# Sums of a layer norm on another engine, centring from PSUM, and a new order of weights and products around it

## The chip, the cores and the metric

One NeuronCore of a Trainium2 chip runs the whole program. The metric is device time in microseconds (us) of one execution. The engines are TensorE (PE, matrix products, its weight loads are PEld), VectorE (DVE), ScalarE (ACT), GpSimd (POOL) and the DMA queues; SP and POOL issue the DMAs here. Each engine runs its own instruction stream in order, and semaphores hold an instruction until what it needs is there.

## The reference

The program is a two-layer decoder trunk on 528 positions (16 learned tokens and 512 inputs) of width 1024. What matters for the change is the shape of a layer:

```python
for l in range(2):
    h = layer_norm(ALPHA * h + 0.5 * swiglu(h, ffn1_wg[l], ffn1_wu[l], ffn1_wd[l]), g[l,0], b[l,0])
    mix = short_conv(h, ...) if l == 0 else forgetting_attention(h, w_q, w_o, k, v, c)
    h = layer_norm(ALPHA * h + mix, g[l,1], b[l,1])
    h = layer_norm(ALPHA * h + 0.5 * swiglu(h, ffn2_wg[l], ffn2_wu[l], ffn2_wd[l]), g[l,2], b[l,2])
    if l == 0: k, v, c = shared_kv(h, kv_w, f_bias)
return h[:, 16:]

def layer_norm(x, g, b):
    mu = mean(x); var = mean((x - mu)**2)
    return (x - mu) * rsqrt(var + 1e-5) * g + b
```

All data are float32. There are six norms. The last one is written in another way and is not touched; the other five, in order of time, are called norm 1 to norm 5: after the first feed-forward block, after the convolution, after the second feed-forward block (its result feeds keys and values), after the third feed-forward block (its result feeds the queries), and after the attention.

## The kernel before, in words

**Layout.** Activations lie transposed: the 1024 features are 8 tiles of 128 partitions (`m` or `k` from 0 to 7), and the positions are the free axis, in two halves `h` of 264 columns in layer 0 and 256 in layer 1. The residual stream is the tile `y`. Every product is made of three float32r matmuls (L243 to L246): weights and activations are split into a high part, rounded on ScalarE (`wh` L132, `xh` L257), and a low part, the remainder, on VectorE (`wl` L134, `xl` L258). A contraction tile of one job is thus three matmuls, and after each the counter `tick` runs; `later(n, fn)` puts work of TensorE n such steps later.

**The order.** The instruction stream of TensorE is the order of the program text. The streams of the other engines are laid out ahead of time by a planner that goes by program order (an earlier line first), readiness in its own simulated time, and dependencies. `tc.high_priority(offset=600)` (L420) moves the end of a norm 600 instructions forward in that order; `tc.issue_after(ins)`, used by `behind` (L112), holds the instructions of the same engine behind `ins`.

**A norm.** `down` (L484) runs the products into `y`: `m` 0 to 2 of both halves, then `m` 3 to 7 of half 0, then `m` 3 to 7 of half 1; each product has 6 contraction tiles in norms 1, 3 and 4 and 8 in norms 2 and 5. Each is added to `y` on VectorE (L502). In `Norm.add` (L395) ScalarE squares the new row of `y`, and GpSimd adds the row to `s1` (L409) and its square to `s2` (L411); row 7 is not added there. `Norm.post` (L413) is placed `LAG[h]` steps behind the last product of its half: TensorE sums row 7 and `s1` into `pd`, and the square of row 7 and `s2` into `pv`, by matmuls with a constant matrix (L419). `finish` (L425) makes the variance `v` (L430), the inverse root `r` by eight VectorE instructions (`rsqrt`, L347), `b = -mean * r` (L434), and then for each pair of tiles `y * r` (L438) and `y + b` (L439), on ScalarE gain and bias (L442), and the split for what comes next (`made`: `xh`, `xl`).

**What comes next.** After norms 1 and 4 it is plain products (`Plain`): in norm 1's case the convolution's three projections `conv_u` (two jobs, `pcc` and `pcv`) and `conv_b` (`pcb`), in norm 4's the queries (`pq`). After norms 2, 3 and 5 it is a unit of gate and up weights, or of key and value weights, whose first 256 columns are computed directly (`Direct.half`, tiles `pc`) for one half after the other; the following units use a scheme with seven products in place of eight, for which sums of weights (L200 to L211) and of activations (`Mixed.sums`, L318) are made on VectorE. `xs.sums()` is held behind the first half's last split (L609). The first product that takes a weight sum of the second unit and `t2` writes `pb`.

**Early weights.** `ahead`, called when the first six products are out (L496), splits the first weights of the next stage; `to.early()`, at the end of `post(0)` (L423), splits more, with `wl` held behind the last split of half 0's activations (`newest`, L446). Buffers: 14 `xtile`s, 5 each of `wh` and `wl`, 3 raw weight buffers of 1 MB, 8 PSUM banks.

Of the kernel before, what the change touches and what calls it, by code (L numbers as in the profile page):

```python
# [34 lines left out]
LEAD = 3  # L35
LAG = (4, 5)
SOON = 600
# [9 lines left out]
def trunk_kernel(  # L47
# [63 lines left out]
    @contextmanager  # L111
    def behind(*after):  # L112


        with ExitStack() as stack:
            for ins in after or newest[-1:]:
                stack.enter_context(tc.issue_after(ins.ins))
            yield

    def split_w(src, shape, home=None):  # L120
# [11 lines left out]
        nc.scalar.copy(a, src)  # L132
        with behind():
            nc.vector.tensor_tensor(b, src, a.bitcast(F32), ALU.subtract)  # L134
# [34 lines left out]
    class Quads:  # L169
# [21 lines left out]
        def sums(self):  # L191
            if "s" in self.got:
                return
            self("a11")
            s = wp.tile([P, KD * P], F32, tag="ws", bufs=1, name="s")
            s = s.rearrange("p (j k n) -> p j k n", j=2, k=KH)
            self.got["s"] = s
            a11, a21, a22 = self.part(0, 0), self.part(1, 0), self.part(1, 1)
            with behind():
                nc.vector.tensor_tensor(s, a21, a22, ALU.add)  # L200
                nc.vector.tensor_tensor(a21, a11, a21, ALU.add)
                nc.vector.tensor_tensor(a11, a11, s, ALU.add)

        def __call__(self, name):
            if name not in self.got:
                if name[0] == "s":
                    self.sums()
                if name == "s4":
                    a12 = self.part(0, 1)
                    with behind():  # L210
                        nc.vector.tensor_tensor(a12, a12, self.part(0, 0), ALU.add)  # L211
# [135 lines left out]
    def rsqrt(v, r, a):  # L347
# [9 lines left out]
        nc.vector.scalar_tensor_tensor(a, v, -10.0 / 3, v, ALU.add, ALU.mult)  # L357
        nc.vector.scalar_tensor_tensor(r, a, 5.0, r, ALU.add, ALU.mult)


    class Norm:
        def __init__(self, layer, i, eps, to):
            self.layer, self.i, self.eps, self.to = layer, i, eps, to
            self.s1, self.s2, self.sq, self.early = {}, {}, {}, {}

# [29 lines left out]
        def add(self, h, m, gather):  # L395

            if h not in self.s2:
                self.early.setdefault(h, []).append((m, gather))
                return
            gather()  # L400
            yv = cols(y, h, self.layer)
# [4 lines left out]
            if m == KD - 1:  # L406
                self.sq[h] = sq
                return
            nc.gpsimd.tensor_tensor(  # L409
                self.s1[h], yv[:, 0, :] if m == 1 else self.s1[h], yv[:, m, :], ALU.add)  # L410
            nc.gpsimd.tensor_tensor(self.s2[h], self.s2[h], sq, ALU.add)  # L411

        def post(self, h):  # L413
# [6 lines left out]
            with tc.high_priority(offset=SOON):  # L420
                self.finish(h, pd, pv)
            if h == 0:
                self.to.early()  # L423

        def finish(self, h, pd, pv):  # L425
            yv = cols(y, h, self.layer)
            w = yv.shape[2]
            v = self.tmp(h, "v", 1)
            nc.scalar.activation(v, pd, AF.Square)
            nc.vector.scalar_tensor_tensor(v, pv, self.eps, v, ALU.add, ALU.subtract)  # L430
            r, a = self.tmp(h, "r", 1), self.tmp(h, "a", 1)
            rsqrt(v, r, a)
            b = self.tmp(h, "b", 1)
            nc.vector.scalar_tensor_tensor(b, pd, -1.0, r, ALU.mult, ALU.mult)  # L434
            rb, bb = (t.unsqueeze(1).broadcast_to([P, 2, w]) for t in (r, b))
            for m in range(0, KD, 2):
                ym = yv[:, m:m + 2, :]
                nc.vector.tensor_tensor(ym, ym, rb, ALU.mult)  # L438
                nc.vector.tensor_tensor(ym, ym, bb, ALU.add)  # L439
                for j in range(m, m + 2):  # L440
# [3 lines left out]
                        scale=vecs[:, c:c + 1], bias=vecs[:, 48 + c:49 + c])  # L444
                last = self.to.made(h, m)
            newest.append(last[1])  # L446

# [130 lines left out]
    class Direct:  # L578
# [6 lines left out]
        def half(self, h, finish):  # L585
            ps = {(j, m): psum(f"pc{j}{m}")[:, :self.w] for m in range(2) for j in range(2)}
            for n in range(2):
                for m in range(2):
                    wh, wl = self.quads(f"a{m + 1}{n + 1}")
                    for j in range(2):  # L590
                        gemms([(ps[j, m], (wh[:, j], wl[:, j]), self.xs[f"b{n + 1}{h + 1}"])],
                              range(KH), start=n == 0, stop=n == 1, chained=True)
            for m in range(2):
# [146 lines left out]
    w_in = [Weights(conv_w_in[0], 0, KD, j * D, KD) for j in range(3)]  # L740
    for j in (1, 2):
        w_in[j].home = {0: xtile}
    xc = Plain(0, lambda: (w_in[1](1), w_in[2](1), w_in[0](0)))
    ffn(0, ffn1_wg[0], ffn1_wu[0], ffn1_wd[0], 0, xs0, xc, ready=f1,
        ahead=lambda: (w_in[1](0), w_in[2](0)))

# [43 lines left out]

    for part, i, h in (
            (conv_u, 0, 0), (conv_u, 1, 0), (conv_b, 0, 0), (conv_u, 0, 1), (conv_b, 0, 1),
            (conv_u, 1, 1), (conv_b, 1, 0), (conv_b, 1, 1)):
        run([part(i, h)])
    for i in range(2, KD):
# [129 lines left out]
    q_w = Weights(attn_w_q[0], 0, KD, 0, H)  # L925
    q_w.home = {m: xtile for m in range(2)}
    xq = Plain(1, lambda: [q_w(m) for m in range(2, 5)])
    ffn(1, ffn1_wg[1], ffn1_wu[1], ffn1_wd[1], 3, xs2, xq, ahead=lambda: (q_w(0), q_w(1)))

# [126 lines left out]
    fetch(0)  # L1056
    project(range(2), [0])
    project(range(2, 5), [0])
    project(range(3), [1])
# [107 lines left out]
```

## Time and profile before

| | |
|---|---|
| median of 3 runs | 1938.0 us (1937.51 to 1941.57) |
| profiled execution, its own time | 1939.81 us |
| its span, first to last instruction | 1938.0 us |
| mean granted TensorE clock | 0.992 |
| TensorE busy | 1882.2 us (97%), 14467 matmuls |
| VectorE busy | 1399.1 us (72%) |
| ScalarE busy | 875.1 us (45%) |
| GpSimd busy | 136.6 us (7%) |

The profile is one execution. A line of the timeline gives start and duration in us, engine, line of the kernel, operation, output and inputs, shapes and count, and in brackets how long the engine idled before and what released it. The granted clock is a share of full speed, averaged over a stretch.

### The profile page before, as it was taken

The page shows a single profiled execution, that of the slowest core. Times are in us where ns is not written, and L with a number is a line of the kernel's source. Part 1 is how long each engine was busy: PE and PEld are TensorE (multiplying, and loading weights), DVE is VectorE, ACT ScalarE, POOL GpSimd, SP SyncE. Part 2 cuts the span into 40 slices and gives each one's busy share as a digit, 9 for nine tenths or more (in the row PEclk, how much of TensorE's full clock was granted, in tenths as well). Part 3 has the DMA queues.
Part 4 walks back from the last instruction along what each step waited for, and adds up shares of the span by engine and source line. Part 5 has one row for each costly group of instructions (what it writes and reads, how often), then busy time and mean ns, then how long its engine had stood idle before and what let it go on. Part 6 is the DMA issues. An engine that isn't in the chain of part 4 may idle for free.

```text
span 1938.0 us, 34607 instructions
## 1 busy us (share of the span) xinstructions
PE 1882.2 (97%) x14467; PEld 1817.5 (94%) x14467; DVE 1399.1 (72%) x2078; ACT 875.1 (45%) x1459; POOL 136.6 (7%) x198
## 2 busy tenths in 40 slices
PE   8999999999998999999899999999999999999997
PEld 7999999999998999999799999999988898989897
DVE  5785858684468776767797787767677788867685
ACT  5353535453245353535454544435455544535360
POOL 0000000300031000000411000000210220000000
PEclk9999999999999999999999999999999999999999
DMA  4333333322330332323224324232514203333241
GB/s 145 99 98 99 99 99 99 98 91 85 109 99 1 123 112 94 110 92 111 92 73 139 121 82 136 83 114 82 181 56 121 94 7 106 108 104 110 88 130 44
DMA packets 180682, 190.43 MB, mean 98 GB/s; under 512 B 5834, under 2 KB 174070, under 8 KB 180526
## 3 DMA queue, kind: packets, MB, share of 16 engines
q1 hardware_dynamic: 178510, 182.74, 29.6%
q0 software_dynamic: 2016, 5.49, 0.8%
q8 instruction: 113, 1.85, 0.4%
q14 instruction: 43, 0.35, 0.1%
HBM read 181.76 MB, written 6.44 MB: 97 GB/s over the span
## 4 chain that ended last, share of the span: by engine, by line
PE 84%; DVE 9%; DMA 2%; ACT 2%; issue 2%; POOL 2%; SPq 0%; DVEq 0%; POOLq 0%; ACTq 0%
PE pb L244 25%; PE pc L244 14%; PE pa L244 6%; PE pq L244 2%; PE pcb L244 2%; PE pcv L244 2%; PE pcc L244 2%; DVE wl L134 1%; DVE xl L258 1%; PE psc L971 1%; PE po L1029 1%; POOL s L411 1%; DVE y L438 1%; POOL s L409 1%; DMA raw<-in_ffn_wu_dram 1%
## 5 line engine op out<-in xcount | busy, mean ns | idle before, releaser
L134 DVE TENSOR_TENSOR wl<-raw,wh 128x1024 fp32r<-128x1024 f32 (+1 forms) x440 | 519.0, 1187 | 196.9 <-ACT wh L132 186.4
L132 ACT CAST wh<-raw 128x1024 fp32r<-128x1024 f32 (+1 forms) x440 | 438.9, 1003 | 469.9 <-PE pc L244 73.5
L244 PE MATMUL pb<-xh,wl 128*128 128x264 f32 (+1 forms) x1408 | 398.4, 283 | 3.8 <-DVE wl L134 3.8
L244 PE MATMUL pb<-xh,wh 128*128 128x264 f32 (+1 forms) x1408 | 398.0, 283 | 0.0
L244 PE MATMUL pb<-xl,wh 128*128 128x264 f32 (+1 forms) x1408 | 397.7, 282 | 0.0
L244 PE MATMUL pc<-xh,wl 128*128 128x264 f32 (+1 forms) x960 | 274.7, 286 | 3.8 <-DVE wl L134 2.8
L244 PE MATMUL pc<-xl,wh 128*128 128x264 f32 (+1 forms) x960 | 273.5, 285 | 2.5 <-DVE xl L258 2.5
L244 PE MATMUL pc<-xh,wh 128*128 128x264 f32 (+1 forms) x960 | 273.0, 284 | 0.0
L244 PEld LDWEIGHTS pb<-xh,wl 128*128 128x128 f32 x1408 | 264.6, 188 | 4.8 <-issue 3.0
L244 PEld LDWEIGHTS pb<-xh,wh 128*128 128x128 f32 x1408 | 265.4, 188 | 0.0
L244 PEld LDWEIGHTS pb<-xl,wh 128*128 128x128 f32 x1408 | 264.5, 188 | 0.3
L244 PEld LDWEIGHTS pc<-xh,wl 128*128 128x128 f32 x960 | 182.3, 190 | 4.7 <-issue 3.1
L244 PEld LDWEIGHTS pc<-xl,wh 128*128 128x128 f32 x960 | 182.4, 190 | 3.5 <-DVE xl L258 3.3
L244 PEld LDWEIGHTS pc<-xh,wh 128*128 128x128 f32 x960 | 182.6, 190 | 0.0
L244 PE MATMUL pa<-xh,wl 128*128 128x264 f32 (+1 forms) x352 | 99.6, 283 | 0.0
L244 PE MATMUL pa<-xh,wh 128*128 128x264 f32 (+1 forms) x352 | 99.5, 283 | 0.0
L244 PE MATMUL pa<-xl,wh 128*128 128x264 f32 (+1 forms) x352 | 99.4, 282 | 0.0
L132 ACT CAST wh<-s 128x1024 fp32r<-128x1024 f32 x44 | 46.1, 1047 | 50.3 <-DVE s L200 12.1
L244 PEld LDWEIGHTS pa<-xh,wh 128*128 128x128 f32 x352 | 66.3, 188 | 0.0
L244 PEld LDWEIGHTS pa<-xl,wh 128*128 128x128 f32 x352 | 66.1, 188 | 0.0
L244 PEld LDWEIGHTS pa<-xh,wl 128*128 128x128 f32 x352 | 66.1, 188 | 0.0
L200 DVE TENSOR_TENSOR s<-raw 128x1024 f32<-128x1024 f32 x44 | 53.6, 1219 | 13.8 <-DMA raw<-in_ffn_wu_dram 13.6
(1920 smaller groups left out, 4541.8 us busy)
## 6 DMA issues: line engine op xcount, KB each, us to landing
raw<-in_ffn_wg_dram SPq DMA_DIRECT2D x88, 512.0 KB, 3.9
raw<-in_ffn_wu_dram SPq DMA_DIRECT2D x88, 512.0 KB, 4.8
raw<-in_ffn_wd_dram SPq DMA_DIRECT2D x48, 768.0 KB, 4.5
raw<-in_conv_w_in_dram SPq DMA_DIRECT2D x12, 1024.0 KB, 4.9
raw<-in_ffn_wd_dram SPq DMA_DIRECT2D x16, 512.0 KB, 3.5
raw<-in_kv_w_dram SPq DMA_DIRECT2D x16, 512.0 KB, 4.7
raw<-in_conv_w_out_dram SPq DMA_DIRECT2D x4, 1024.0 KB, 5.5
raw<-in_attn_w_q_dram SPq DMA_DIRECT2D x4, 1024.0 KB, 6.4
```

The source lines that it names most:

```text
L132: nc.scalar.copy(a, src)
L134: nc.vector.tensor_tensor(b, src, a.bitcast(F32), ALU.subtract)
L200: nc.vector.tensor_tensor(s, a21, a22, ALU.add)
L244: nc.tensor.matmul(ps, lhsT=a[:, k, :], rhs=b(k), start=start and k == ks[0] and j == 0, stop=stop and k == ks[-1] and j == 2, skip_group_ ...
L258: return a, nc.vector.tensor_tensor(dst_l, src32, dst_h.bitcast(F32), ALU.subtract)
L409: nc.gpsimd.tensor_tensor(self.s1[h], yv[:, 0, :] if m == 1 else self.s1[h], yv[:, m, :], ALU.add)
L411: nc.gpsimd.tensor_tensor(self.s2[h], self.s2[h], sq, ALU.add)
L438: nc.vector.tensor_tensor(ym, ym, rb, ALU.mult)
L971: nc.tensor.matmul(ps, lhsT=q[:, M + t * P:M + (t + 1) * P], rhs=kt[:, a:b], start=True, stop=True)
L1029: nc.tensor.matmul(po[:, q0:S], lhsT=vt[:, j * P:(j + 1) * P], rhs=pT[j // 2][:, j % 2, q0:S], start=j == 0, stop=False)
```

## The change

1. The additions into `s1` and `s2` go from GpSimd to VectorE. For half 1, once half 0 is finished, they are held behind the last instruction of half 0's inverse root (`self.chain`).
2. `finish` no longer makes `b`. It subtracts the mean, read from PSUM (`pd`), from each pair of tiles of `y`, and then multiplies by `r`. The first pair's subtraction stands ahead of `v`; the others are held behind the inverse root. `pd` stays in use until the last of them.
3. `to.early()` is called when the last product of half 1 has been added to `y`, and its VectorE part is held behind that addition and behind half 1's last addition into `s2`.
4. `Direct.half` runs its four jobs of a contraction half side by side over each contraction tile, where it ran two pairs of jobs each over all its tiles. The convolution runs `conv_u` and `conv_b` of one tile together (three jobs), half by half; the queries run in threes and twos. The weights for these are split early, in `xtile`s where they did not use them before.
5. `LAG` of half 1 goes from 5 to 8 steps.

`behind()` without arguments no longer means the newest split; its callers pass that themselves.

```diff
-LAG = (4, 5)
+LAG = (4, 8)
@@ behind
-            for ins in after or newest[-1:]:
+            for ins in after:
@@ split_w (and in the same way Quads.sums, Quads.__call__)
-        with behind():
+        with behind(*newest[-1:]):
@@ rsqrt
-        nc.vector.scalar_tensor_tensor(r, a, 5.0, r, ALU.add, ALU.mult)
+        return nc.vector.scalar_tensor_tensor(r, a, 5.0, r, ALU.add, ALU.mult)
@@ Norm.__init__
-            self.s1, self.s2, self.sq, self.early = {}, {}, {}, {}
+            self.s1, self.s2, self.sq, self.early, self.last = {}, {}, {}, {}, {}
+            self.chain = []
@@ Norm.add
-            gather()
+            last = gather()
+            if h == 1 and m == KD - 1:
+                with behind(last, self.last[h]):
+                    self.to.early()
...
-            nc.gpsimd.tensor_tensor(
-                self.s1[h], yv[:, 0, :] if m == 1 else self.s1[h], yv[:, m, :], ALU.add)
-            nc.gpsimd.tensor_tensor(self.s2[h], self.s2[h], sq, ALU.add)
+            with behind(*self.chain):
+                nc.vector.tensor_tensor(
+                    self.s1[h], yv[:, 0, :] if m == 1 else self.s1[h], yv[:, m, :], ALU.add)
+                self.last[h] = nc.vector.tensor_tensor(self.s2[h], self.s2[h], sq, ALU.add)
@@ Norm.post
-            if h == 0:
-                self.to.early()
@@ Norm.finish
+            mean = pd.unsqueeze(1).broadcast_to([P, 2, w])
             nc.scalar.activation(v, pd, AF.Square)
+            nc.vector.tensor_tensor(yv[:, 0:2, :], yv[:, 0:2, :], mean, ALU.subtract)
             nc.vector.scalar_tensor_tensor(v, pv, self.eps, v, ALU.add, ALU.subtract)
             r, a = self.tmp(h, "r", 1), self.tmp(h, "a", 1)
-            rsqrt(v, r, a)
-            b = self.tmp(h, "b", 1)
-            nc.vector.scalar_tensor_tensor(b, pd, -1.0, r, ALU.mult, ALU.mult)
-            rb, bb = (t.unsqueeze(1).broadcast_to([P, 2, w]) for t in (r, b))
+            last = rsqrt(v, r, a)
+            self.chain = [last]
+            rb = r.unsqueeze(1).broadcast_to([P, 2, w])
             for m in range(0, KD, 2):
                 ym = yv[:, m:m + 2, :]
+                if m:
+                    with behind(last):
+                        nc.vector.tensor_tensor(ym, ym, mean, ALU.subtract)
                 nc.vector.tensor_tensor(ym, ym, rb, ALU.mult)
-                nc.vector.tensor_tensor(ym, ym, bb, ALU.add)
...
@@ Direct.half
             for n in range(2):
+                jobs = []
                 for m in range(2):
                     wh, wl = self.quads(f"a{m + 1}{n + 1}")
-                    for j in range(2):
-                        gemms([(ps[j, m], (wh[:, j], wl[:, j]), self.xs[f"b{n + 1}{h + 1}"])],
-                              range(KH), start=n == 0, stop=n == 1, chained=True)
+                    jobs += [(ps[j, m], (wh[:, j], wl[:, j]), self.xs[f"b{n + 1}{h + 1}"])
+                             for j in range(2)]
+                gemms(jobs, range(KH), start=n == 0, stop=n == 1, chained=True)
@@ convolution
-    for j in (1, 2):
+    for j in range(3):
         w_in[j].home = {0: xtile}
-    xc = Plain(0, lambda: (w_in[1](1), w_in[2](1), w_in[0](0)))
+    xc = Plain(0, lambda: (w_in[1](1), w_in[2](1), w_in[0](1)))
     ffn(0, ffn1_wg[0], ffn1_wu[0], ffn1_wd[0], 0, xs0, xc, ready=f1,
-        ahead=lambda: (w_in[1](0), w_in[2](0)))
+        ahead=lambda: (w_in[1](0), w_in[2](0), w_in[0](0)))
...
-    for part, i, h in (
-            (conv_u, 0, 0), (conv_u, 1, 0), (conv_b, 0, 0), (conv_u, 0, 1), (conv_b, 0, 1),
-            (conv_u, 1, 1), (conv_b, 1, 0), (conv_b, 1, 1)):
-        run([part(i, h)])
+    for h in range(2):
+        for i in range(2):
+            run([conv_u(i, h), conv_b(i, h)])
@@ queries
-    q_w.home = {m: xtile for m in range(2)}
-    xq = Plain(1, lambda: [q_w(m) for m in range(2, 5)])
-    ffn(1, ffn1_wg[1], ffn1_wu[1], ffn1_wd[1], 3, xs2, xq, ahead=lambda: (q_w(0), q_w(1)))
+    q_w.home = {m: xtile for m in range(3)}
+    xq = Plain(1, lambda: [q_w(m) for m in range(3, 5)])
+    ffn(1, ffn1_wg[1], ffn1_wu[1], ffn1_wd[1], 3, xs2, xq, ahead=lambda: [q_w(m) for m in range(3)])
...
-    project(range(2), [0])
-    project(range(2, 5), [0])
+    project(range(3), [0])
+    project(range(3, 5), [0])
```

## Rows read from the trace of the kernel before

**Rows 1.** The page's busy time: engine, us (share), instructions.
```profile
PE 1882.2 (97%) x14467; PEld 1817.5 (94%) x14467; DVE 1399.1 (72%) x2078; ACT 875.1 (45%) x1459; POOL 136.6 (7%) x198
```

**Rows 2.** TensorE's waits: on what, us in total, times, longest.
```profile
PE pd L419 <- POOL s L409: 8.7, 5, 4.0
```

**Rows 3.** Timeline of VectorE in norm 1, from the last weight splits on.
```profile
366.31 4.08 DVE L134 TENSOR_TENSOR wl<-raw,wh 128x768 fp32r<-128x768 f32 x3
370.32 0.41 DVE L502 TENSOR_TENSOR y<-y,pd__4102 128x264 f32<-128x264 f32 x1
370.66 0.41 DVE L502 TENSOR_TENSOR y<-y,pd__4158 128x264 f32<-128x264 f32 x1
...
381.02 0.43 DVE L430 SCALAR_TENSOR_TENSOR v<-pv,v 128x264 f32<-128x264 f32 x1 [6.31 <-PE pv L419]
...
382.04 0.42 DVE L352 TENSOR_TENSOR a<-r 128x264 f32<-128x264 f32 x1
382.50 0.87 DVE L353 SCALAR_TENSOR_TENSOR a<-a,v 128x264 f32<-128x264 f32 x1
...
387.19 1.42 DVE L438 TENSOR_TENSOR y<-y,r 128x528 f32<-128x528 f32 x2
```

**Rows 4.** Stretches: from:to, length, busy us (instructions) by engine, clock, DMA.
```profile
951.00:1000.00 49.00, 44.46 (x343) 42.22 (x343) 47.55 (x79) 28.63 (x55) 10.80 (x14) 1.00 0.06 23
1561.00:1610.00 49.00, 46.48 (x372) 45.71 (x370) 45.74 (x77) 30.31 (x57) 6.34 (x7) 0.97 0.00 1
```

**Rows 5.** Timeline of VectorE at the end of norm 2.
```profile
587.01 3.45 DVE L134 TENSOR_TENSOR wl<-raw,wh 128x1024 fp32r<-128x1024 f32 x2
...
594.85 0.43 DVE L430 SCALAR_TENSOR_TENSOR v<-pv,v 128x264 f32<-128x264 f32 x1 [4.05 <-PE pv L419]
...
599.28 1.32 DVE L438 TENSOR_TENSOR y<-y,r 128x528 f32<-128x528 f32 x2
```

**Rows 6.** Timeline of VectorE at the program's start.
```profile
16.30 1.22 DVE L134 TENSOR_TENSOR wl<-raw,wh 128x1024 fp32r<-128x1024 f32 x1
```

**Rows 7.** Timeline of TensorE around norm 1.
```profile
379.31 0.71 PE L419 MATMUL pd<-s,ones_all 128*128 128x264 f32 x2 [3.15 <-POOL s L409]
...
391.44 0.39 PE L244 MATMUL pcc<-xh,wl 128*128 128x264 f32 x1 [1.00 <-ACT xh L257]
...
397.90 0.61 PE L419 MATMUL pv<-s,ones_all 128*128 128x264 f32 x2
```

**Rows 8.** Timeline of VectorE in norm 3, as rows 3.
```profile
933.98 5.76 DVE L134 TENSOR_TENSOR wl<-raw,wh 128x768 fp32r<-128x768 f32 x4
...
957.23 1.42 DVE L438 TENSOR_TENSOR y<-y,r 128x528 f32<-128x528 f32 x2
```

**Rows 9.** Timeline of TensorE around norm 3.
```profile
947.71 1.20 PE L419 MATMUL pd<-s,ones_all 128*128 128x264 f32 x2 [3.99 <-POOL s L409]
...
967.95 0.61 PE L419 MATMUL pv<-s,ones_all 128*128 128x264 f32 x2
...
981.20 0.39 PE L244 MATMUL pc<-xl,wh 128*128 128x264 f32 x1 [0.86 <-DVE xl L258]
```

**Rows 10.** Timeline of TensorE around norm 4.
```profile
1404.92 0.70 PE L419 MATMUL pd<-s,ones_all 128*128 128x256 f32 x2 [0.80 <-POOL s L409]
...
1416.78 0.39 PE L244 MATMUL pq<-xh,wl 128*128 128x256 f32 x1 [1.05 <-ACT xh L257]
...
1424.05 0.70 PE L419 MATMUL pv<-s,ones_all 128*128 128x256 f32 x2
```

**Rows 11.** Timeline of TensorE at norm 2 and the weight sum behind it.
```profile
590.86 1.25 PE L419 MATMUL pd<-y,ones_all 128*128 128x264 f32 x2 [3.65 <-DVE y L502]
...
629.84 0.36 PE L244 MATMUL pb<-xh,wl 128*128 128x264 f32 x1 [1.20 <-DVE wl L134]
```

**Rows 12.** Timeline of TensorE at norm 5 and the weight sum behind it.
```profile
1575.27 0.70 PE L419 MATMUL pv<-s,ones_all 128*128 128x256 f32 x2 [2.30 <-POOL s L411]
...
1611.23 0.35 PE L244 MATMUL pb<-xh,wl 128*128 128x256 f32 x1 [1.45 <-DVE wl L134]
```

More of the change, by code (lines that the diff above doesn't have):

```diff
@@ L198, in sums @@
             a11, a21, a22 = self.part(0, 0), self.part(1, 0), self.part(1, 1)
-            with behind():
+            with behind(*newest[-1:]):
                 nc.vector.tensor_tensor(s, a21, a22, ALU.add)
@@ L209, in __call__ @@
                     a12 = self.part(0, 1)
-                    with behind():
+                    with behind(*newest[-1:]):
                         nc.vector.tensor_tensor(a12, a12, self.part(0, 0), ALU.add)
@@ L444, in finish @@
                         scale=vecs[:, c:c + 1], bias=vecs[:, 48 + c:49 + c])
-                last = self.to.made(h, m)
-            newest.append(last[1])
+                made = self.to.made(h, m)
+            newest.append(made[1])
     def lagged(n, head, layer, group=1, tail=0):
```

## Prediction

> **What bounds the kernel now.** I read the page's busy times first: TensorE is busy 97% of a span of 1938.0 us [rows 1], so time is to be had only where it waits or runs slowly. The list of TensorE's waits comes second: its longest entry is the mean's product `pd` waiting for GpSimd's `s1`, 8.7 us in all [rows 2]. VectorE's timeline comes third: in norm 1 it idles 6.31 us before `v` [rows 3], but in the long stretches behind norms 3 and 5 it is busy 47.55 and 45.74 of 49.00 us [rows 4]: there its work is as long as TensorE's. So VectorE work that is added before `v` is nearly free, and behind it costs something. Around each norm the reader is to see two holes in TensorE's timeline: one at `post` of half 0, while `pd` waits for a sum, and one where the next stage begins and `post` of half 1 follows.
>
> **A second effect in the same rows.** While GpSimd runs a sum, VectorE is slowed: L353 takes 0.87 us in norm 1 [rows 3], while the same kind of instruction with GpSimd at rest takes 0.43 (594.85, rows 5); two weight splits take 3.45 us [rows 5], where one alone takes 1.22 [rows 6], a factor of 0.71. Moving the sums removes this.
>
> **Part 1, sums of half 0.** 12 additions of half 0 and 4 of half 1's rows 1 and 2 come to VectorE. A sum of two tiles in SBUF of 264 columns isn't there before; nearest are L352 at 0.42 us and, since instructions overlap, the additions L502, which start 0.34 us apart [rows 3]. Bounds 0.34 and 0.42, the doubled 0.87 being excluded with GpSimd idle; I take 0.34.
> Norm 1: from 366.31 VectorE has three splits (4.08 disturbed, 2.9 by the factor above), 16 sums (5.4) and five additions into `y` (1.7): 10.0 us, done at 376.3. Before, `pd` went on at 379.31 [rows 7]; `v` followed 1.71 us later at 381.02 [rows 3] and moves to some 378.0, 3.0 us earlier.
> Norm 3: from 933.98 four splits (5.76, undisturbed 4.1; rows 8), 16 sums and five additions: 11.2 us, the last sum at 945.2. `pd` went on at 947.71, and its product ran at 1.20 us [rows 9] against 0.71 [rows 7]. With 1.5 us from the last sum to `v`, that is 946.7.
> Norms 2 and 5 have longer products, so more room; norm 4's wait of 0.80 us [rows 10] goes. If sums go ahead of the weight splits of products 5 to 7, TensorE waits for a split instead; I charge 0.24 us a norm, 1.2 in all.
>
> **Part 2, chain from `v` to the next stage.** In norm 1 `v` at 381.02 leads to the first `y * r` at 387.19, 6.17 us [rows 3]; undisturbed it is 594.85 to 599.28, 4.43 [rows 5]. Without `b` (0.35) that is 4.08, with two additions into `y` between (0.68) some 4.75: 1.4 us less. Then two multiplications, 1.42 us [rows 3], and an addition of some 0.67 stood before ScalarE; now one multiplication of 0.67 does, 1.4 less. The first subtraction has its place while `pv` is being made, so it costs nothing; without that cover it is 0.67 on the chain. From `v` to the first product of the next stage 10.4 us (381.02 to 391.44, rows 7) become 7.6, which in norm 1 is 385.6. TensorE is through half 1's products at 390.44 - 3.0 = 387.4, so the waits at the start of a stage (1.00 in norm 1, 1.05 in norm 4; rows 7 and 10) go.
>
> [...] The addition that reads PSUM takes 0.41 us, the one from SBUF alone 0.42 [rows 3]: I charge nothing for the operand. [...]
>
> **Part 3, half 1's sums and `post(1)`.** From the first `y * r` on VectorE has seven multiplications and subtractions (4.5 us; two take 1.32, rows 5), four `xl` of the same width (2.5), three additions (1.0) and the eight sums of rows 3 to 6 (2.7): 10.7 us, then 0.8 until `pv` is complete. Behind the held sums on VectorE are queued the early splits, for products that come 5.8 us (48 matmuls) later, and half 1's own chain. `post(1)` now stands 24 matmuls behind the stage's start, not 15: nine more (1.1 us at 0.12 each; the mean over all kinds is 1882.2 / 14467 = 0.130, rows 1) are done when it ends.
> Norm 1: 378.0 + 4.75 + 11.5 = 394.2; before, 397.90 + 0.61 = 398.5 [rows 7]. With the 1.1: **5.4 us**, parts 1 and 2 included. TensorE still waits some 1.8 us there.
> Norm 3: the first `y * r` comes at 951.4, not 957.23 [rows 8], and `post(1)` ends at 962.9, not 968.56 [rows 9]: 5.7 + 1.1 = 6.8, and a later wait for half 1's `xl` (0.86, rows 9, and one of 0.54) goes: 8.2. But VectorE is full from 951 to 1000 [rows 4]. Its work ends earlier only by those 5.8, less 2.7 for sums, plus 1.6 for one `b` and undisturbed splits, plus half of the idle 1.45: 5.4; the weight sums' splits had some 0.6 us to spare: **6.0 us**.
> Norm 4: `v` at 1404.92 - 0.80 + 1.7 = 1405.8, first `y * r` 1410.4, `post(1)` done at 1421.7 (256 columns) against 1424.75 [rows 10]: 3.1 + 1.1 = **4.2 us**.
>
> **Part 4, early weights.** In norm 2 two splits of 3.45 us stood before half 1's last addition [rows 5]; `pd` waited 3.65 us for it, and its product then took 1.25 us [rows 11]. That stall goes. What is late next is the weight sum's split, for which TensorE waited 1.20 us until 629.84 [rows 11]. It moves with VectorE: the idle 4.05 us before `v` [rows 5] are filled by the two splits, and some 1.0 comes off for `b` and undisturbed instructions: **5.0 us**.
> In norm 5 GpSimd's sum costs 2.30 us [rows 12], but the split of 1611.23, already 1.45 us late [rows 12], follows a VectorE that is 93% busy [rows 4]. Sums add 2.7 us to it; doubled instructions (0.9), `b` twice (0.7), two undisturbed splits (1.0), `xl` (0.6) and 1.0 of idle time come off: **1.5 us**.
>
> **Part 5, products side by side.** They want a pair of activation tiles each 2.2 us (three jobs) or 2.9 (four), where ScalarE makes one each 1.5 us, so waits for `xl` inside a stage go; that is in the ends above. At the program's start the second weights are wanted earlier, behind one split (1.22 us, rows 6); I charge half, 0.6. `pd` is held some 4 us longer; by my count of banks enough are free when the next stage takes its own, so nothing; were it not so, TensorE would wait up to those 4 us in the three short norms.
>
> **Sum.** 5.4 + 5.0 + 6.0 + 4.2 + 1.5 = 22.1, less 1.2 and 0.6: 20.3 us. The profiled execution's own time, 1939.81 (span 1938.0), becomes 1919.5; the median of the runs, 1938.0, is 1.8 lower, so I forecast **1918 us** for the median.
>
> **Rivals.**
> (a) VectorE is the next bound in all five norms. For it: [rows 4]. Against it: 6.31 us idle in norm 1 [rows 3]. If half 1's sums follow all other work and early splits come before `v`, norms 1, 3 and 4 lose 3 us each, 9 of the 20: 1927, at worst 1933.
> (b) More is won: the planner finds room for the weight sums, and norms 2, 3 and 5 get all of TensorE's own waits and slow products (7.8, 8.2 and 5.5, not 12.5 together): 9 more, 1909.
> (c) The change doesn't do what it says: the wait for `s` on GpSimd becomes as long a wait for `s` on VectorE, because the planner puts every split first. Then the chain's 2.8 us in three norms remain, and 2.7 us of sums eat them: 1936 to 1940. Against it: the idle 6.31 us [rows 3].
> (d) Slower, by one mechanism: sums go ahead of the splits that products 5 to 7 of the same half wait for. 16 sums are 5.4 us; a stall of that length is also followed by slow products, as in norm 2 (1.25 for 0.71, some 2 us in all). 7.4 us in each of five norms is 37, less 22: 1953. It decides from 4.4 us a norm on. Against it: only the three splits of 366.31 are still due when the first sum can start [rows 3].
>
> **How the numbers follow.** Forecast, 1912 to 1925: 0.60; (a) 0.18, (b) 0.09, (c) 0.06, (d) 0.07. No change means within 0.2%, 3.9 us, about what a measurement can tell from nothing. Faster 0.87, same 0.06, slower 0.07. The range 1908 to 1932 takes in (b), nearly all of (a), and the upper price of the sums (0.08 x 24 x 5 = 10 us on VectorE, half of it behind `v`).
>
> **What would show it.** GpSimd's busy time near 30 us; in norms 1 and 3 `pd` waits under 2 us for `s`; `v` to the first `y * r` some 4.75 us; no wait at the first product of a stage; `post(1)` in norms 1, 3 and 4 with 1 to 2.5 us of waiting for VectorE; in norm 2 none for `y`; the weight sum's splits 2 us or more late in norms 2 and 5. It is wrong if TensorE waits for `wl` in the products into `y`, or if the ends of `post(1)` move by less than 2 us.

## The result, and the profile after

The changed kernel takes **1923.7 us** (median; 1922.97 to 1924.85, 4 runs) against 1939.8 for the kernel before in the same comparison (1937.51 to 1944.81, 4 runs): ratio 0.9914, 95% interval 0.9892 to 0.9936, 16 us less. The prediction was 1918 us, 1908 to 1932. The differences in us between two versions below are of medians; by the ratios they come out within 1.5 us of these. The profiled execution took 1922.97 us, span 1921.2.

The page's busy times after, columns as in [rows 1]:

```profile
PE 1878.4 (98%) x14467; PEld 1818.5 (95%) x14467; DVE 1417.4 (74%) x2188; ACT 875.6 (46%) x1459; POOL 25.4 (1%) x78
```

120 sums left GpSimd (198 to 78 instructions). On VectorE they start 0.34 us apart, 41 us in all, yet VectorE is busy only 18.3 us more: ten `b` went (4 us), and what GpSimd had slowed runs undisturbed again (L353 in norm 1 takes 0.43 us for 0.87, the 440 splits of L134 509.1 us for 519.0).

TensorE's longest waits after, columns as in [rows 2]; those left out lie in the first 17 us of the program:

```profile
PE pd L424 <- DVE y L508: 9.8, 6, 2.3
...
PE pc L244 <- ACT sg L669: 3.2, 1, 3.2
PE pb L244 <- DVE wl L134: 3.0, 2, 1.9
...
PE pc L380 <- ACT first L376: 1.0, 1, 1.0
```

The 8.7 us for GpSimd [rows 2] are gone, but `pd` now waits 9.8 us for VectorE, and a wait for a `silu` on ScalarE, which the prediction didn't have, is new. TensorE's gaps fell from 44.1 to 31.4 us (summed over its whole timeline); the other 4 us or so are slow products that became fast (6.4 us for 10.7, by the estimate of the last section).

To see where the time came from I cut both timelines at the one-matmul shift of half 0 that begins each norm (L380 after; 359.17 us before). After:

```profile
356.09 0.28 PE L380 MATMUL pc<-first,ones_pre 128*128 128x264 f32 x1
...
542.40 0.29 PE L380 MATMUL pc<-first,ones_pre 128*128 128x264 f32 x1
...
917.09 0.28 PE L380 MATMUL pc<-first,ones_pre 128*128 128x264 f32 x1
...
1371.31 0.28 PE L380 MATMUL pc<-first,ones_pre 128*128 128x256 f32 x1
...
1517.55 0.28 PE L380 MATMUL pc<-first,ones_pre 128*128 128x256 f32 x1
```

The lengths between these cuts, us, one profile each; the last stretch ends with TensorE's last product ("sums only" is the kernel before with the sums moved, "lag + mixed" the best version; both are below):

| stretch | before | after | gain | predicted | sums only | lag + mixed |
|---|---|---|---|---|---|---|
| start | 359.17 | 356.09 | 3.1 | -0.6 | 359.70 | 356.67 |
| norm 1 and on | 188.96 | 186.31 | 2.7 | 5.4 | 185.61 | 183.75 |
| norm 2 and on | 378.69 | 374.69 | 4.0 | 5.0 | 377.89 | 373.51 |
| norm 3 and on | 460.75 | 454.22 | 6.5 | 6.0 | 456.18 | 454.41 |
| norm 4 and on | 147.37 | 146.24 | 1.1 | 4.2 | 144.52 | 142.74 |
| norm 5 and on | 391.43 | 392.28 | -0.9 | 1.5 | 392.40 | 388.96 |

(The predicted column leaves out the 1.2 us charged over all norms.) Norms 2 and 3 came near the forecast, norm 1 gave half of it, norm 4 a quarter, and norm 5 lost. Some of each difference is TensorE's clock, which differs by execution (a mean of 0.990 to 0.994 in 15 executions of the kernel before; see the last section).

TensorE at the norms after, to be held against [rows 7, 9 and 10]:

```profile
373.95 0.68 PE L424 MATMUL pd<-y,ones_all 128*128 128x264 f32 x2 [1.03 <-DVE y L508]
...
375.93 0.71 PE L424 MATMUL pv<-sq,ones_all 128*128 128x264 f32 x2 [0.85 <-ACT sq L409]
...
391.73 0.71 PE L424 MATMUL pd<-y,ones_all 128*128 128x264 f32 x2 [2.25 <-DVE y L508]
...
935.91 0.71 PE L424 MATMUL pd<-y,ones_all 128*128 128x264 f32 x2 [1.41 <-DVE y L508]
952.58 0.71 PE L424 MATMUL pd<-y,ones_all 128*128 128x264 f32 x2 [2.19 <-DVE y L508]
...
1404.81 1.22 PE L424 MATMUL pd<-y,ones_all 128*128 128x256 f32 x2 [2.27 <-DVE y L508]
```

At `post(0)` the waits of 3.15 and 3.99 us are down to 1.03 and 1.41, and for half 0's last addition into `y`, not for a sum; in norm 1 `pv` waits another 0.85 for the square. The waits at the first product of the next stage (1.00 in norm 1, 1.05 in norm 4) are gone. Each `post(1)` of norms 1, 3 and 4 waits 2.2 us for half 1's last addition.

VectorE in norm 1 after, against [rows 3]:

```profile
373.38 0.42 DVE L508 TENSOR_TENSOR y<-y,pd__4236 128x264 f32<-128x264 f32 x1
375.59 1.22 DVE L134 TENSOR_TENSOR wl<-raw,wh 128x1024 fp32r<-128x1024 f32 x1 [1.78 <-ACT wh L132]
376.73 0.69 DVE L434 TENSOR_TENSOR y<-y,pd 128x528 f32<-128x528 f32 x1
377.34 0.42 DVE L435 SCALAR_TENSOR_TENSOR v<-pv,v 128x264 f32<-128x264 f32 x1
...
378.81 0.43 DVE L353 SCALAR_TENSOR_TENSOR a<-a,v 128x264 f32<-128x264 f32 x1
...
381.72 0.70 DVE L444 TENSOR_TENSOR y<-y,pd 128x528 f32<-128x528 f32 x1
382.33 1.32 DVE L445 TENSOR_TENSOR y<-y,r 128x528 f32<-128x528 f32 x2
383.57 1.31 DVE L444 TENSOR_TENSOR y<-y,pd 128x528 f32<-128x528 f32 x2
...
391.25 0.42 DVE L508 TENSOR_TENSOR y<-y,pd__4401 128x264 f32<-128x264 f32 x1
```

L353 takes 0.43 us where it took 0.87. From `v` to the first `y * r` it is 4.99 us, where it was 6.17. But `v` itself came late: a weight split of 1.22 us stands in front of the subtraction, and VectorE waited 1.78 us for its cast. ScalarE at the same place:

```profile
374.51 1.04 ACT L132 CAST wh<-raw 128x1024 fp32r<-128x1024 f32 x1 [1.90 <-DMA raw<-in_conv_w_in_dram]
375.46 0.42 ACT L409 ACTIVATE sq<-y 128x264 f32<-128x264 f32 x1
```

The cast waited 1.90 us for its weights, and the square that `pv` needs stood behind it. This is the third of the weights that the change splits ahead (`w_in[0](0)`).

Behind norm 5, ScalarE and then TensorE:

```profile
1582.71 0.61 ACT L257 CAST xh<-t 128x512 fp32r<-128x512 f32 x1
...
1584.17 1.65 ACT L257 CAST xh<-t 128x512 fp32r<-128x512 f32 x3
1585.73 0.63 ACT L669 ACTIVATE sg<-pc 128x256 f32<-128x256 f32 x2
```

```profile
1586.15 0.58 PE L244 MATMUL pc<-xh,wl 128*128 128x256 f32 x1 [3.19 <-ACT sg L669]
1586.53 0.41 PE L244 MATMUL pc<-xl,wh 128*128 128x256 f32 x1
```

`p5` needs two PSUM banks. Side by side, all four banks of half 1 end together, and the `silu` that frees one stands behind casts of `Mixed.sums`. After the wait the products run at half clock (0.50 from 1586 to 1592 us; see the last section).

### The profile page after: what moved, and what is told of

The parts are those of the page before. It is cut to its first block, busy times and chain, and to the rows that moved or that the text cites. A ratio compares the mean times of both kernels' runs of the same rounds, so it can differ in the third digit from the quotient of the medians.

```text
span 1921.2 us, 34484 instructions
## 1 busy us (share of the span) xinstructions
PE 1878.4 (98%) x14467; PEld 1818.5 (95%) x14467; DVE 1417.4 (74%) x2188; ACT 875.6 (46%) x1459; POOL 25.4 (1%) x78
## 4 chain that ended last, share of the span: by engine, by line
PE 83%; DVE 11%; DMA 3%; ACT 2%; issue 1%; SPq 0%; DVEq 0%; ACTq 0%
PE pb L244 26%; PE pc L244 14%; PE pa L244 6%; PE pcb L244 2%; PE pcv L244 2%; PE pcc L244 2%; PE pq L244 2%; DVE wl L134 2%; DVE xl L258 1%; ACT wh L132 1%; PE psc L977 1%; PE po L1035 1%; DVE y L445 1%; DVE y L508 1%; DVE s L416 1%
## 5 line engine op out<-in xcount | busy, mean ns | idle before, releaser
L134 DVE TENSOR_TENSOR wl<-raw,wh 128x1024 fp32r<-128x1024 f32 (+1 forms) x440 | 509.1, 1164 | 189.6 <-ACT wh L132 181.4
```

## The experiments

Each kernel was timed beside the kernel before on its own chip; ratios are to that. To compare two of them, ratios serve better than medians.

**Sums back on GpSimd** (`e1`), one part undone.

```
-            with behind(*self.chain):
-                nc.vector.tensor_tensor(   # s1, and s2 alike
+            nc.gpsimd.tensor_tensor(
...
```

The holds go with them: early weights are held behind half 1's last addition into `y` alone.

> The changed kernel with only the additions into s1 and s2 back on GpSimd (without the holds, which are VectorE's). Theory 1, the sums are the main source of the gain, by being late and by slowing VectorE: the waits of pd for s come back (some 3 us in norm 1, 4 in norm 3, 2 in norm 5), GpSimd is busy 137 us, and the kernel takes 6 to 10 us more than the changed one, 1930 to 1934. Theory 2, the gain comes from the products side by side and from the later post(1): GpSimd's late sums are then covered, at most 3 us more, under 1927.

Measured 1934.4 us, ratio 0.9970 (0.9958 to 0.9982): 10.7 us more than the changed kernel. Theory 1 holds, theory 2 falls. The waits for `s` are 4.15 us in norm 1 and 3.98 in norm 3 as expected, but the third, of 2.11, is in norm 4 and not in norm 5. Its longest wait of TensorE, and a sum on GpSimd with the VectorE instruction that it slows (0.86 us, 0.43 in the changed kernel), in norm 1:

```profile
PE pd L423 <- POOL s L413: 10.2, 3, 4.1
```

```profile
382.90 0.88 POOL L413 TENSOR_TENSOR s<-s,y 128x264 f32<-128x264 f32 x1 [4.23 <-DVE y L507]
...
383.20 0.86 DVE L353 SCALAR_TENSOR_TENSOR a<-a,v 128x264 f32<-128x264 f32 x1
```

**`Direct.half` in turn again** (`e2`): the loop over `m` and `j` calls `gemms` for one job at a time, as before.

> The changed kernel with only Direct.half as it was, pairs of jobs in turn (the convolution and the queries stay side by side). Theory 1, side by side is worth little here and costs a wait for PSUM banks: the wait of 3.2 us behind norm 5 and the slow matmuls after it go (5 us), the start is 1.7 us earlier; in norm 3 waits for xl of 1.4 us come back: 2 to 5 us less than the changed kernel, 1919 to 1922. If the stretch at half clock at 72 to 80 us of the kernel before comes back as well, its 3 us come on top: about no change. Theory 2, the gain comes from side by side: 4 us more or above, 1928 and up.

Measured 1923.1, ratio 0.9907 (0.9892 to 0.9923): no difference that can be told. The stretch behind norm 5 is 3.3 us shorter (388.97) and has no wait for `sg`, so that much of theory 1 is seen; its start took 358.70 and norm 1 189.79, which took it back. The start has the half clock behind 72 us that the expectation named (0.65 from 76 to 80 us), and in norm 1 the products behind `post(0)` and behind `post(1)` both ran at half clock (0.66 from 378.7 to 383.7 us, 0.72 from 394 to 399), where the changed kernel's did not (1.00 from 374 to 400).

**Old centring** (`e3`): `b` made, `y * r`, `y + b`.

> The changed kernel with only the centring as it was (b made, y times r, plus b). Theory 1, a shorter chain from v to the next stage: the waits at the first product of a stage come back in norms 1, 3 and 4 (about 1 us each, and post(1) as much later): 2 to 4 us more, 1926 to 1928. Theory 3, VectorE's total work is the limit in every norm: only b's 10 instructions of 0.35 us come on top, half of them where it counts: at most 1.5 us more.

Measured 1929.8, ratio 0.9952 (0.9936 to 0.9967): 6.1 us more, above both expectations. Norms 1, 2 and 3 take 2.0, 0.7 and 2.2 us more, norm 4 0.6; the start, which has no norm in it, 1.6. But in the start and norm 1 this profile has products at half clock where the changed kernel's profile has none (a granted clock of 0.90 from 76 to 84 us, and in norm 1 of 0.72 from 394 to 400 us, by which it loses some 1.7 us; 1.00 in both for the changed kernel), while norms 2 and 5 of the changed kernel have some (0.72 from 618 to 624 us, 0.50 from 1586 to 1592). What theory 1 named is not seen: at the first product of a stage no wait of 1 us is back, only waits of 0.4 to 0.5 us for `xl`, in norms 2 and 5 for `xh` too, and `post(1)` waits 2.1 us as in the changed kernel. So the cost is measured, and where it arises stays open.

**Early weights back at `post(0)`** (`e4`).

```
-            if h == 1 and m == KD - 1:
-                with behind(last, self.last[h]):
-                    self.to.early()
...
+            if h == 0:            # at the end of post
+                self.to.early()
```

> The changed kernel with only to.early() back at the end of post(0). Theory 1: the stall of 3.65 us at norm 2's pd comes back with slow matmuls behind it, a smaller one in the other norms: 4 to 7 us more, 1928 to 1931. Theory 3, VectorE's total work is the limit: the same two splits only stand elsewhere, the weight sum's split is late by as much as before: at most 2 us more.

Measured 1941.3, ratio 1.0006 (0.9997 to 1.0015): 17.6 us more, far beyond both, and all of the change's gain. These three undone parts cost 10.7 + 6.1 + 17.6 = 34 us, twice what the whole change gave, so they aren't independent. The waits say where:

```profile
PE pd L421 <- DVE y L507: 20.9, 8, 5.6
```

Norm 2's stall is the smaller matter (1.60 us there); `post(1)` waited 5.64, 4.46 and 4.52 us in norms 1, 3 and 4. The kernel before, with early weights at the same place, waited under 0.7 us for `pd` in each of them.

**Sums only** (`e8`): the kernel before with `nc.gpsimd` turned to `nc.vector` in the two lines.

> The kernel before with only the additions into s1 and s2 moved to VectorE. If the parts' gains add up, it gains what taking this part out of the changed kernel cost (10.7 us): 1927 to 1931. If the parts need each other, because the early weights at the end of post(0) stand ahead of half 1's additions on VectorE: the waits for s in half 0 go (10 us with the slow product behind them), but post(1) waits 4 to 6 us in norms 1, 3 and 4 as it did with early weights at post(0): 1936 to 1943, no change.

Measured 1929.6, ratio 0.9948 (0.9935 to 0.9960): 10.8 us less than before. The sums alone give two thirds of the gain. In norms 1 and 4 they alone gain 3.4 and 2.9 us (the table), more than the whole change in its profile (2.7 and 1.1). Norm 4's 1.1 comes with products at half clock (1404 to 1409 us at 0.66, a loss of 1.6 us by the estimate of the last section), which the kernel before has there too (1418 to 1424 us at 0.72); in `e2` and `e5`, with the changed code there, norm 4 takes 144.44 and 144.49, as much as with the sums only. So in norm 4 the rest of the change gains nothing, rather than loses. Norms 2 and 5 keep stalls of 3.3 us at `pd`, but `post(1)` waits only 0.25 us in norms 1 and 4, and that with early weights at `post(0)`.

**The hold taken away** (`e10`), and with early weights at `post(0)` besides (`e11`). The first edit is

```
-            self.chain = [last]
```

> The changed kernel without the hold of half 1's sums behind half 0's inverse root. Theory 4, the hold leaves the gaps of the dependent chain empty (its instructions start 0.46 us apart where independent ones start 0.34 apart) and puts 4 us of sums ahead of half 1's last addition into y: without it post(1) no longer waits 2.2 us in norms 1, 3 and 4, the chain from v to the first y times r grows by some 1 us, and the kernel takes 2 to 5 us less than the changed one, 1919 to 1922. Rival, the hold pays: half 0's chain is longer, the next stage starts 1 us late in three norms: 1 to 4 us more, 1925 to 1928.

> The same without the hold, and to.early() back at the end of post(0). Theory 4, early weights cost 17.6 us at post(0) only because of the hold (held sums, then early splits, then the last additions): here only the stalls of 3.3 us at pd in norms 2 and 5 come back, 5 to 8 us more than without the hold alone, 1926 to 1930. Rival, the early splits alone do it: post(1) waits 4 us or more in norms 1, 3 and 4 without the hold as well, 1936 or more.

Measured 1925.8, ratio 0.9929 (0.9916 to 0.9943), and 1941.1, ratio 1.0006 (0.9996 to 1.0016). Theory 4 falls twice. The first time is in the rival's range, but the intervals of the changed kernel and of `e10` overlap, so whether the hold pays can't be told. The chain did grow, from 4.38 to 5.31 us (`v` to the subtraction behind the inverse root in norm 1), but the last addition of half 1 started at 391.63, where with the hold it was 391.25 (35.3 and 35.2 us behind the shift): VectorE has the same work before it in either order. `post(1)` still waits 1.9 us in norms 1, 3 and 4. And without the hold early weights cost 15.3 us, nearly as much as with it.

**The old centring on top of `e11`** (`e13`): of the norm's edits only the sums are left.

> The changed kernel without the hold, with early weights back at the end of post(0), and with the old centring too: of the norm's edits only the sums on VectorE are left (the side by side products and LAG 8 stay). Theory 5, early weights at post(0) cost 17.6 us only because the shorter chain of the new centring lets them overtake half 1's last addition into y: with the longer chain the splits fall behind it again, post(1) waits under 1.5 us in norms 1, 3 and 4, the stalls of 3.3 us in norms 2 and 5 stay, and the kernel takes 1927 to 1932, some 10 us less than with the new centring. Rival, centring and early weights are independent: its 6.0 us come on top of 1941, 1945 or more.

Measured 1932.2, ratio 0.9964 (0.9951 to 0.9976): taking a second improvement out made the kernel 9.0 us faster. Theory 5 holds: `post(1)` waits at most 0.86 us in norms 1, 3 and 4. The time is just above what it said, though the stalls in norms 2 and 5 are smaller than it said (2.2 us, not 3.3). VectorE at half 1's last addition in norm 1, first with the new centring (`e11`), then with the old:

```profile
394.65 3.49 DVE L134 TENSOR_TENSOR wl<-raw,wh 128x1024 fp32r<-128x1024 f32 x3
...
398.40 0.43 DVE L506 TENSOR_TENSOR y<-y,pd__4413 128x264 f32<-128x264 f32 x1
```

```profile
396.29 0.42 DVE L504 TENSOR_TENSOR y<-y,pd__4415 128x264 f32<-128x264 f32 x1
396.62 0.70 DVE L258 TENSOR_TENSOR xl<-y,xh 128x528 fp32r<-128x528 f32 x1
397.24 2.35 DVE L134 TENSOR_TENSOR wl<-raw,wh 128x1024 fp32r<-128x1024 f32 x2
```

Early splits are held behind the last `xl` of half 0. With the old centring that comes after half 1's last addition. The new one makes half 0 done sooner, in the planner's time as well, and three splits of 3.5 us slip in front of the addition. `post(1)` waits 5.27 us instead of 0.85.

**Pairs in turn over the second contraction half** (`e5`), and **the `silu` first** (`e6`), both against the wait behind norm 5:

```
+                for group in [jobs[0] + jobs[1]] if n == 0 else jobs:     # e5
+                    gemms(group, range(KH), start=n == 0, stop=n == 1, chained=True)
...
+                with tc.high_priority(offset=SOON):                       # e6, around sg
```

> The changed kernel with Direct.half side by side over the first contraction half only; over the second one pair of jobs after the other, so that the first two banks of half 1 come free 2.9 us earlier. If the wait behind norm 5 is one for PSUM banks that end together: it goes (3.2 us), and so do the slow matmuls behind it (2.6 us): 3 to 6 us less than the changed kernel, 1918 to 1921. If it is ScalarE's queue alone, whose silu stands behind casts that wait for VectorE whenever the bank ends: the wait stays at 2 us or more, and the time within 1.5 us of 1924.

> The changed kernel with the silu of the directly computed columns and the multiplication behind it moved 600 instructions forward in the planner's order, so that ScalarE runs the silu before the casts of the sums of activations. If the wait behind norm 5 comes from the silu's place in ScalarE's queue: it falls below 1 us, 3 to 5 us less than the changed kernel, 1919 to 1921. If the banks end too late in any case: a silu and a multiplication (some 1 us) still stand between the last product and the bank, the wait stays above 2 us and the time at 1924.

Measured 1924.1, ratio 0.9918 (0.9904 to 0.9931), and 1923.4, ratio 0.9916 (0.9903 to 0.9930). The expected 3 to 6 us are not in the times. In the profiles the mechanism shows: without the four banks ending together no wait for `sg` is left, with the `silu` first 1.42 us of it, and the stretch behind norm 5 takes 389.09 and 389.47 where it took 392.28. So banks and queue both have a part. The medians don't show the 3 us; in `e5`'s profile the start (359.61) and norm 1 (187.92) took them back.

**`post(1)` six steps later in norms 1, 3 and 4** (`e7`).

```
+                    later(14 if h and norm.i in (0, 2, 3) else LAG[h], ...)
```

> The changed kernel with post(1) six steps later (18 matmuls, 2.2 us) in norms 1, 3 and 4, where TensorE waits 2.2 us for the last addition into y. Theory 1, the chain is the limit there: the three waits go, 4 to 6 us less than the changed kernel, 1918 to 1920. Theory 3, VectorE's total work is the limit behind these norms: the time that TensorE saves is waited for at the next xl or weight sum's split, at most 1.5 us less.

Measured 1921.7, ratio 0.9908 (0.9893 to 0.9923), 2.0 us less: between the two, and by the intervals not to be told from the changed kernel. The profile parts them by norm: 184.10 in norm 1 (2.2 less than the changed kernel) and 142.74 in norm 4 (3.5 less, of which up to 1.6 is the half clock that the changed kernel's profile has there), but 455.51 in norm 3 (1.3 more), where the 2.19 us are waited for at the next half's `xh`:

```profile
963.65 0.39 PE L244 MATMUL pc<-xh,wl 128*128 128x264 f32 x1 [2.19 <-ACT xh L257]
```

Behind norm 3 VectorE is the limit: half 1's `v` stands 37.6 us behind the shift, in the changed kernel 37.8, so the wait only moved. Behind norms 1 and 4 it isn't. Whether it is VectorE's total work, or only that two early splits of 1.2 us (at 953.41 and 955.51) stand ahead of and inside half 1's chain there, no run here parts.

**Both, where they help** (`e12`): the later `post(1)` in norms 1 and 4, the pairs in turn behind norm 5 alone.

> The changed kernel with post(1) six steps later in norms 1 and 4 alone (norm 3 gave the wait back at the next xh), and pairs in turn over the second contraction half behind norm 5 alone. If both are independent of each other, from the sections of the single runs: norm 1 2.2, norm 4 1.7 to 3.5, norm 5 3.2 us: 7 us less than the changed kernel, 1916 to 1919. If what they save is waited for elsewhere, as the medians of the single edits (2.0 and -0.4) say: 1920 to 1923.

Measured **1915.5 us** (1913.19 to 1919.33), ratio 0.9873 (0.9858 to 0.9887): 8 us less than the changed kernel, whose interval it doesn't touch, and the fastest version here. The profiles' stretches foretold it, the single medians (2.0 less and 0.4 more) didn't. A part of it is the clock: by the estimate of the last section it costs 1.7 us in this profile and 6.4 in the changed kernel's. Its longest waits, those of norms 1 and 4 at `post(1)` and the one for `sg` no longer among them:

```profile
PE pd L424 <- DVE y L508: 5.0, 4, 2.2
PE pb L244 <- DVE wl L134: 4.6, 3, 1.9
```

## Why the prediction was right, and where its sizes were not

The direction and the mechanism were right. Most of what the prediction said would show did: GpSimd at 25 us, `pd` under 2 us at `post(0)`, 4.99 us from `v` to the first `y * r`, no wait at a stage's first product, 2.2 us at `post(1)` in norms 1, 3 and 4, none for `y` in norm 2, the weight sum's split 1.90 us late there. In norm 5 no weight sum's split is late. The time is 6 us above the forecast: 4 us because 16 came off and not 20, the rest because the kernel before has a median of 1939.8 in this comparison and 1938.0 in the one that the forecast started from. In the table the five norms give 13.4 us where 22.1, less 1.2, were forecast; 3.1 come from the start, where a loss was forecast. The terms:

- **Part 1, norm 1: `v` 3.0 us earlier.** Counted from the shift, `v` stood at 21.85 us before (381.02 - 359.17) and at 21.25 after (377.34 - 356.09): 0.6 earlier. With the sums only it is 19.72 (379.42 - 359.70), 2.1 earlier. So the sums gave 2.1 of the 3.0, and 1.5 us went elsewhere. About 1.0 of it went to a step priced nowhere: the third weight split ahead for the side by side convolution, whose cast waits for its DMA in front of the square. I counted the activation tiles of Part 5, not its weights. With this split and the old centring (`e3`) `v` stood at 20.67 (378.33 - 357.66). The other 0.6 lie between `e3` and the changed kernel: the cast waited 1.90 us for its DMA where in `e3` it waited 1.59, and the first subtraction, behind the late split, no longer had the cover for which it was priced at nothing. `v` with the sums only, then in `e3`:

```profile
379.42 0.43 DVE L430 SCALAR_TENSOR_TENSOR v<-pv,v 128x264 f32<-128x264 f32 x1 [2.27 <-PE pv L419]
```

```profile
378.33 0.43 DVE L433 SCALAR_TENSOR_TENSOR v<-pv,v 128x264 f32<-128x264 f32 x1 [0.38 <-PE pv L424]
```

- **Part 3, norms 1 and 4 (5.4 and 4.2).** The wait at `post(1)` was foreseen in norm 1 (1.8, measured 2.25), but as a small rest. It is a cost of the change: sums only has 0.25 there. `e7` and `e12` show that those 2 us can be had by a later `post(1)`; LAG 8 was at most six steps short. In norm 4 the products after the wait also ran at half clock (0.66 from 1404 to 1409 us), as they did in the kernel before (0.72 from 1418 to 1424); no term had this.
- **Norm 3 (6.0).** Measured 6.5, with 1.2 of it a wait at the following shift that was not in the term, and with products at half clock in the kernel before (1.20 for 0.71, [rows 9]; a clock of 0.66 from 947 to 952 us) that the changed kernel doesn't have there (1.00 from 930 to 993). The wait that `e7` found fits the limit named for it, VectorE's work, without proving that it is the total.
- **Part 4, norm 2 (5.0).** The 3.65 us stall and the half clock behind it (0.50 from 590 to 596 us) went; 4.0 came off, with products at half clock behind the 1.90 us wait in their place (0.72 from 618 to 624 us).
- **Norm 5 (1.5).** The two waits of [rows 12] went, and -0.9 came out, since a new wait of 3.19 us took their place. Part 5 counted the banks for `pd` and found enough; it did not ask when the four banks of `Direct.half` itself end, nor what stands ahead of the `silu` on ScalarE.
- **Start (-0.6).** It was 3.1 us shorter, but it differs by run: 356.1 to 361.0 over the ten profiles that have the changed kernel's `Direct.half`, 358.7 to 359.7 over the four that don't. Most of the difference lies around 74 us. There ScalarE's cast of a weight waited 3.31 us for its DMA in the kernel before and 1.17 in the changed one, TensorE waited for `hh` behind it (1.67 us before), and then ran at half clock (0.50 from 76 to 80 us). Before, then after, columns as in [rows 4]:

```profile
76.00:84.00 8.00, 8.00 (x50) 8.00 (x50) 4.95 (x10) 1.05 (x1) 0.00 (x0) 0.70 0.02 7
```

```profile
76.00:84.00 8.00, 8.00 (x68) 8.00 (x67) 7.49 (x13) 2.11 (x2) 0.00 (x0) 1.00 0.04 15
```

  Nine kernels, the changed one among them, have the same order of instructions on VectorE and ScalarE over the first 350 us; five of these have the half clock (`e3`, `e4`, `e7`, `e11`, `e13`: 0.60 to 0.90 from 76 to 84 us), four don't (1.00). So up to 3 of the 16 us of the table are the luck of one execution. The four profiles with another `Direct.half` at the start all have it (0.70 to 0.82), so a part may still belong to the change.

Of the rivals, (a), VectorE as the next bound in all five norms, is seen in norm 3 and not in norms 1 and 4, where a later `post(1)` gains; in norm 2 the 1.90 us wait for a split points to it, and in norm 5 it was not tested. (d) shows in small: a product ahead of norm 3's `post(0)` waited 0.70 us for a split. What no term or rival held is that the parts lean on each other: moving the early weights was priced at norm 2's stall, some 5 us, while with the new centring in place it is worth 17.6 (15.3 without the hold), because without it the shorter chain would put the early splits ahead of half 1's last addition.

Two subtractions that read PSUM (L444, 528 columns) take 1.31 us, two multiplications from SBUF alone (L445) 1.32: no price of a PSUM source is seen, and the prediction charged none. In `e1` L353 takes 0.86 us beside a sum on GpSimd, with the sums on VectorE 0.43.

## What to carry to other kernels

Moving short sums off an engine that slows its neighbour (L353 0.87 us beside a sum on GpSimd, 0.43 without) can be worth more than the wait that the profile names, here 10.8 us for 8.7. When a chain is made shorter, look at everything that is held behind its end: it moves forward too, and may overtake what the path needs. Before products are run side by side, write down when each PSUM bank then ends, who empties it, what stands ahead of that in its queue, and which extra weights have to be ready.

## What the runs showed of the hardware

TensorE's clock after a wait, which no term had for the waits that the change brought, differs by run. The columns here are the stretch, its length, then busy us (instructions) of PE, PEld, DVE, ACT and POOL, the granted clock, and DMA share and GB/s; changed kernel, norm 4's `post(1)`, then behind norm 5 ahead of the wait for `sg` and after it:

```profile
1404.00:1409.00 5.00, 4.19 (x15) 3.54 (x16) 3.82 (x9) 1.13 (x3) 0.00 (x0) 0.66 0.24 75
...
1579.00:1582.00 3.00, 3.00 (x28) 3.00 (x27) 3.00 (x4) 2.15 (x3) 0.00 (x0) 1.00 0.00 0
1586.00:1592.00 6.00, 5.85 (x27) 5.85 (x28) 4.97 (x11) 2.71 (x8) 0.00 (x0) 0.50 0.00 0
```

After 3.19 us of waiting 27 products took 6 us at a granted clock of 0.50 where 28 had taken 3 us at 1.00: by this the wait cost nearly its own length once more. Where the clock is lower in the kernel before and in the changed one, it is 0.50 in the steps of 1 us inside; 0.66 or 0.72 is the mean of a stretch that has both 0.50 and 1.00. TensorE's busy time times the missing share of the clock, summed over the profile in steps of 1 us, is an estimate of what the lower clock costs: 10.7 us before, 6.4 after, 8.1 with the sums only, 1.7 in the best version. By stretch, in the order of the table, it is 3.1, 0, 2.7, 1.6, 1.6 and 1.7 before and 0, 0, 1.7, 0, 1.6 and 3.1 after. In norm 1 `post(1)` waits the same 2.2 us in the changed kernel and in `e2`, with the same code there; the product behind it took 0.71 us in the one and 1.17 in the other, and that stretch 186.31 and 189.79 us; in `e2` the products behind `post(0)` ran slow as well (a clock of 0.66 from 378.7 to 383.7 us). So one profile of a stretch carries some 2 to 3 us of such chance, and a single edit of that size can't be read from it. Behind norm 5 the wait of 3.19 us and the lower clock after it come to 6.3 us by the estimate; with that wait gone (`e5`) the stretch was 3.2 us shorter, so that taking such a wait away saves more than the wait is not shown.
